# Masked-autoencoder loss: other column pieces and other PSUM tiles in the last columns

## The chip, the cores and the metric

The kernel runs on one core of a Trainium2 chip. The metric is the device time of one execution in microseconds (us). Of the kernel before, six runs are shown: 76.96 to 77.12, with a median of 77.03.

## The reference

`pred` and `target` are float32 arrays of 32 x 147 x 768 (batch, masked patches, values of a patch). Each patch of `target` is normalised by its own mean and variance, the squared difference to `pred` is averaged over the 768 values, and then over the 147 patches. The result is 32 numbers.

```python
mean = target.mean(axis=-1, keepdims=True)
var = target.var(axis=-1, keepdims=True)
target = (target - mean) / np.sqrt(var + 1e-6)
loss = np.mean((pred - target) ** 2, axis=-1)
return loss.mean(axis=-1).astype(np.float32)
```

## The kernel before

**Tiling.** Four partitions hold the patches of one batch entry, so 32 entries fill 128 partitions. A partition holds up to 37 patches, one after the other; the kernel calls each a column, 768 values wide. Columns 0 to 35 fill all 128 partitions. Column 36, called `REST`, has 96. `KM` is 36, `half` is 384, `BANK` is 512 and `D` is 768.

**Loads.** The list `stream` (lines 54 to 78) sets the order of the loads. Target comes in pieces of four columns, `pred` in pieces of four, then of two (columns 24 to 31), then of one (32 to 34); column 35 comes in two pieces of 384 values. Two target pieces are issued by SP, all else by POOL, whose transfers convert float32 to bfloat16. POOL issues a load between other work, in the order that the planner sets.

**Statistics and normalisation.** DVE takes mean and variance of a target column (lines 161 and 162), ACT the square root (185), DVE the reciprocal (191). POOL writes the normalised column into a tile `s` (line 211).

**Difference and square.** A unit is a stretch of one or two columns that is finished by one path. On the ACT path PE multiplies `s` by minus the identity into PSUM (`sub_target`, the operation `subt`, a subtraction), then adds `pred` by the identity (`add_pred`, the operation `pred`, an addition); both matmuls are on line 228. ACT squares the PSUM tile in place and sums it (line 249; the sum is read out by an ACTIVATION_READ_ACCUMULATOR). On the DVE path DVE subtracts (line 265) and squares with a sum (line 269), or leaves the square to ACT ("DVE+ACT").

From column 26 on each unit is divided. Columns 26 and 27, 28 and 29, 30 and 31 are pairs, and 32 to 35 are single. ACT takes the first part of a column's values, DVE the rest. The part of ACT is 512 values wide up to column 33, and 384 for columns 34 and 35 (lines 87 to 90). A pair's part is two matmuls of 512, a single column's is one.

**PSUM.** Whole pairs of columns up to 23 and `REST` use a pool of two tiles of three banks. When the first part is to be subtracted, that pool is closed and a pool `parts` of three tiles of two banks takes its place (lines 231 to 242). Every part takes the next of the three tiles, so it can be written only when the part three before it was squared: 32 waits for 26 and 27, 33 for 28 and 29, 34 for 30 and 31, and 35 for 32. The sum over partitions, `acc`, has a bank of its own.

**Order.** All operations are put into a list with an estimated duration, the operations that they need, a rank, and, where they need a transfer, its estimated landing. A planner (lines 336 to 356) takes again and again the operation that can start first by these estimates, and issues it. This fixes the program order of every engine. The estimates fix no time: on the chip an engine does its instructions in that order, each when its operands are there.

**End.** Squares of the last six units are summed one by one. The earlier ones stand side by side in `rl` and are reduced on DVE (`rl_sum`, line 321). PE multiplies each vector of sums by a mask into `acc` (line 328), DVE copies it (359), and SP stores it (360).

Of the kernel before, what the change touches and what calls it, by code (L numbers as in the profile page):

```python
# [7 lines left out]
F32 = mybir.dt.float32  # L8
# [6 lines left out]
def kernel(  # L15
# [9 lines left out]
    B, N, D = pred.shape  # L25
    eps = 1e-6
    P = 128
    J = P // B
    KJ = (N + J - 1) // J
    KM = N - (J - 1) * KJ  # L30
    assert KJ == KM + 1
    RP = B * (J - 1)
    half = D // 2
    BANK = 512
# [19 lines left out]
    def piece(kind, c0, c1, d0=0, d1=D, q="sw"):  # L54
        stream.append((kind, c0, c1, d0, d1, q))
# [18 lines left out]
        piece("p", c, c + 2)  # L74
    for c in range(32, 35):
        piece("p", c, c + 1)
    piece("p", KM - 1, KM, 0, half)
    piece("p", KM - 1, KM, half, D)


    groups = [(0, 1), (2, 3), (REST,)] + [tuple(range(c, c + 4)) for c in range(4, KM, 4)]
# [2 lines left out]
    units = [((c, c + 1), 0, D, "ACT" if c < 14 else "DVE+ACT") for c in range(0, 24, 2)]  # L84
    units.insert(2, ((REST,), 0, D, "ACT"))
    units += [((24,), 0, D, "DVE"), ((25,), 0, D, "DVE+ACT")]
    for u in [(c, c + 1) for c in range(26, KM - 4, 2)] + [(c,) for c in range(KM - 4, KM - 1)]:
        m = BANK if u[0] < KM - 2 else half
        units += [(u, 0, m, "ACT"), (u, m, D, "DVE")]
    units += [((KM - 1,), 0, half, "ACT"), ((KM - 1,), half, D, "DVE")]  # L90

# [3 lines left out]
    def op(name, engine, dur, needs, fn, rank=0.0, early=0.0):  # L97
        by_name[name] = len(ops)
        ops.append((name, engine, dur, needs, fn, rank, early))
# [17 lines left out]
    for i, (kind, c0, c1, d0, d1, q) in enumerate(stream):  # L117
        w = (c1 - c0) * (d1 - d0)
# [4 lines left out]
        k = len(lanes[q])  # L123
# [6 lines left out]
    ident = singles.tile([P, P], BF16)  # L130
# [71 lines left out]
    def normalise(u, c):  # L202
        n = rows_of(c)
        if c == u[0]:
            s = work.tile([P, 2 * D], BF16, name="s")
            for m, cc in enumerate(u):
                sbuf[cc] = (s, m * D)
        s, so = sbuf[c]
        (_, _, til, o), = tbuf[c]
        r, nm = rs[c]  # L210
        pin(nc.gpsimd.tensor_scalar(out=s[:n, so:so + D], in0=til[:n, o:o + D], scalar1=nm, scalar2=r,  # L211
                                    op0=ALU.add, op1=ALU.mult))


    zs = {}
# [5 lines left out]
    def product(u, d0, w, src, so, eye, first):  # L221
        n, z = rows_of(u[0]), zs[u, d0]

        runs = [(0, so, w)] if w % D == 0 else [(k * BANK, so + k * D, w // len(u)) for k in range(len(u))]
        for zo, o, e in runs:
            for a in range(0, e, BANK):
                b = min(e, a + BANK)
                pin(nc.tensor.matmul(z[:n, zo + a:zo + b], eye[:n, :n], src[:n, o + a:o + b],  # L228
                                     start=first, stop=not first))

    def sub_target(u, d0, w):
        if u in pairs_pe:
            zs[u, d0] = pools["pairs"].tile([P, 3 * BANK], F32, name="z")
            pairs_pe.remove(u)
        else:
            if "parts" not in pools:

                pools["stack"].close()
                pools["parts"] = ctx.enter_context(tc.tile_pool(name="parts", bufs=3, space=bass.MemoryType.PSUM))
            zs[u, d0] = pools["parts"].tile([P, 2 * BANK], F32, name="zp")  # L240
        s, so = sbuf[u[0]]
        product(u, d0, w, s, so + d0, nident, True)

    def add_pred(u, d0, w):
        product(u, d0, w, *pred_of(u[0], d0), ident, False)

    def square_act(u, d0, w, dest):
        n, z = rows_of(u[0]), zs[u, d0]
        pin(nc.scalar.activation(out=z[:n, :w], in_=z[:n, :w], func=ACTF.Square, accum_out=dest[:n]))  # L249

    def difference(u, d0, w):

        z = zs[u, d0] = diffs.tile([P, 2 * D], BF16, name="zd")
        s, so = sbuf[u[0]]
        til, o = pred_of(u[0], d0)
        K, e = len(u), w // len(u)
        if e == D:
            x, y, v = z[:, :w], til[:, o:o + w], s[:, so:so + w]
        elif K == 1:
            x, y, v = z[:, :w], til[:, o:o + w], s[:, so + d0:so + d0 + w]  # L260
        else:
            x = z[:, :w].rearrange("p (k d) -> p k d", d=e)
            y = til[:, o - d0:o - d0 + K * D].rearrange("p (k d) -> p k d", d=D)[:, :, d0:d0 + e]
            v = s[:, so:so + K * D].rearrange("p (k d) -> p k d", d=D)[:, :, d0:d0 + e]
        pin(nc.vector.tensor_tensor(out=x, in0=y, in1=v, op=ALU.subtract))  # L265

    def square_dve(u, d0, w, dest):
        z = zs[u, d0][:, :w]
        pin(nc.vector.scalar_tensor_tensor(out=z, in0=z, scalar=1.0, in1=z, op0=ALU.mult, op1=ALU.mult,  # L269
                                           accum_out=dest))  # L270
# [6 lines left out]
    n_pairs = len(pairs_pe)  # L277
    pools = {"stack": ExitStack()}
    pools["pairs"] = pools["stack"].enter_context(tc.tile_pool(name="psum", bufs=2, space=bass.MemoryType.PSUM))
    finals = []  # L280
    early_ops, users, dusers, dprev, seen = [], [], [], [], set()
    for k, (u, d0, d1, eng) in enumerate(units):
        w = len(u) * (d1 - d0)
        arrive = max(t for (kk, c, d), t in land.items() if kk == "p" and c in u and d < d1)
        norms = [("norm", c) for c in u]
        for c in u:
            if c not in seen:
                op(("norm", c), "POOL", 1.02, [("recip", group_of[c])], lambda u=u, c=c: normalise(u, c), rank=k)
                seen.add(c)
        if k < len(units) - tail:  # L290
            if u[0] == REST:
                dest = singles.tile([P, 1], F32, name="rl_rest")
                finals.append((("sq", k), dest, mask_rest, RP))
            else:
                dest = rl[:, len(early_ops):len(early_ops) + 1]
                early_ops.append(("sq", k))
        else:
            dest = singles.tile([P, 1], F32, name=f"rl{k}")
            finals.append((("sq", k), dest, mask, P))
        if eng in ("DVE", "DVE+ACT"):  # L300
            op(("diff", k), "DVE", 0.57 * w / D + 0.05, norms + dusers[-5:-4] + dprev[-1:], lambda u=u, d0=d0, w=w: difference(u, d0, w), rank=-2.0,
               early=arrive)
            dusers.append(("sq", k))
            dprev.append(("diff", k))
            if eng == "DVE":
                op(("sq", k), "DVE", 1.0 * w / D, [("diff", k)],
                   lambda u=u, d0=d0, w=w, dest=dest: square_dve(u, d0, w, dest), rank=-1.0)
            else:
                op(("sq", k), "ACT", 0.65 * w / D + 0.22, [("diff", k)],
                   lambda u=u, d0=d0, w=w, dest=dest: square_act(u, d0, w, dest), rank=k)  # L310
            continue
        op(("subt", k), "PE", 0.37 * w / D, norms + (users[-2:-1] if len(users) < n_pairs else users[n_pairs - 1:n_pairs] + users[n_pairs:][-3:-2]) + ["ident"],
           lambda u=u, d0=d0, w=w: sub_target(u, d0, w), rank=k + 0.0)
        op(("pred", k), "PE", 0.37 * w / D, [("subt", k)], lambda u=u, d0=d0, w=w: add_pred(u, d0, w), rank=k,
           early=arrive)
        op(("sq", k), "ACT", 0.65 * w / D + 0.22, [("pred", k)],
           lambda u=u, d0=d0, w=w, dest=dest: square_act(u, d0, w, dest), rank=k)
        users.append(("sq", k))

    acc = psum1.tile([1, B], F32)  # L320
    op("rl_sum", "DVE", 0.2, early_ops, lambda: pin(nc.vector.tensor_reduce(
# [18 lines left out]
    while left:  # L340
        best = None
        for i in left:
            name, engine, dur, needs, fn, rank, early = ops[i]
# [8 lines left out]
        name, engine, dur, needs, fn, rank, early = ops[i]  # L352
# [43 lines left out]
```

## Time and profile before

| what | before |
|---|---|
| median of six runs | 77.03 us |
| the profiled execution | 77.12 us |
| its span, first to last instruction | 75.4 us |
| PE busy | 28.9 us |
| DVE busy | 56.4 us |
| ACT busy | 30.3 us |
| POOL busy | 53.7 us |
| loads | 15.41 MB written, 28.90 MB read at 383 GB/s |
| mean granted TensorE clock | 0.769 |

The span ends with the last instruction; the time also holds what lies around the program. Busy time is a sum over the whole span, so an engine can be half idle and yet set the end. A line of the timeline gives the start, the duration, the engine, the line of the kernel and the operation, what it writes and reads, and in brackets how long its engine was idle before it and what ended that. The names of buffers leave their numbers out: `zp` is any tile of the pool `parts`, `zd` the output of the DVE's subtraction. The ends of matmuls are modelled: several in a row follow each other sooner than their durations say.

### The profile page before, as it was taken

The numbers are of one execution on the slowest core, as the hardware profiler recorded it, in microseconds if no ns is written. First come the engines' busy times: TensorE is split into PE (matmuls) and PEld (weight loads), VectorE is DVE, ScalarE is ACT, GpSimd is POOL, SyncE is SP. The second block draws the span as 40 slices with busy tenths as digits, with TensorE's granted clock in tenths as the row PEclk, the third lists the DMA queues.
The fourth block names the chain that finished last, engine by engine and source line by source line (L and its number), as shares of the span: only waits on it lengthen the run. The fifth ranks groups of instructions, "written<-read, shape, count | busy, mean of one in ns | idle before, by whom it ended". The sixth has DMA issues, their size and how long they took to land.

```text
span 75.4 us, 551 instructions
## 1 busy us (share of the span) xinstructions
PE 28.9 (38%) x81; PEld 8.3 (11%) x82; DVE 56.4 (75%) x155; ACT 30.3 (40%) x65; POOL 53.7 (71%) x75
## 2 busy tenths in 40 slices
PE   0000001472005876004986006770719300379860
PEld 0000000110002131001121002120103000112230
DVE  0000699999999979999759999375797289998860
ACT  5100021200102893020690010880099969965760
POOL 6998006997399949698989898997695999800000
PEclk9999999999999999995557965555555555555598
DMA  0799999999999999999999999999999999999700
GB/s 0 215 417 324 254 240 218 191 239 209 215 215 212 209 219 215 228 209 212 215 212 212 219 212 225 215 209 215 215 215 215 199 215 212 212 204 204 109 0 0
DMA packets 3685, 15.41 MB, mean 204 GB/s; under 512 B 418, under 2 KB 1154, under 8 KB 3554
## 3 DMA queue, kind: packets, MB, share of 16 engines
q0 software_dynamic: 3424, 13.52, 88.6%
q1 hardware_dynamic: 258, 1.87, 6.8%
q14 instruction: 3, 0.02, 0.1%
HBM read 28.90 MB, written 0.00 MB: 383 GB/s over the span
## 4 chain that ended last, share of the span: by engine, by line
DMA 60%; POOL 22%; DVE 5%; issue 3%; PE 3%; ACT 3%; ACTq 1%; POOLq 0%
DMA t<-in_target_dram 31%; DMA p<-in_pred_dram 29%; POOL s L211 15%; DVE st L161 4%; POOL p L111 4%; ACT zp L249 3%; PE zp L228 3%; POOL t L111 2%; ACTq L391 1%; DVE mv L162 1%; POOL nident L139 0%; POOL ident L139 0%; PE acc L328 0%; DVE ob L359 0%; POOL nident L138 0%
## 5 line engine op out<-in xcount | busy, mean ns | idle before, releaser
L161 DVE BATCH_NORM_STATS2 st<-t 128x6 f32<-128x384 bf16 (+2 forms) x74 | 36.2, 531 | 10.5 <-DMA t<-in_target_dram 10.5
L211 POOL TENSOR_SCALAR s<-t,nm,r 128x768 bf16<-128x768 bf16 (+2 forms) x37 | 38.3, 1043 | 5.6 <-DVE r L191 4.9
L228 PE MATMUL z<-p,ident 128*128 128x512 bf16 (+2 forms) x23 | 10.1, 596 | 19.1 <-DMA p<-in_pred_dram 19.1
L228 PE MATMUL z<-s,nident 128*128 128x512 bf16 (+2 forms) x23 | 9.8, 536 | 15.9 <-POOL s L211 14.3
L249 ACT ACTIVATE z<-z 128x1536 f32<-128x1536 f32 (+1 forms) x8 | 10.9, 1357 | 12.2 <-PE z L228 12.2
L185 ACT ACTIVATE r<-mv,eps_t 128x4 f32<-128x4 f32 (+2 forms) x11 | 3.2, 292 | 27.1 <-DVE mv L162 26.4
L265 DVE TENSOR_TENSOR zd<-p,s 128x1536 bf16<-128x1536 bf16 (+4 forms) x14 | 9.6, 702 | 3.6 <-DMA p<-in_pred_dram 3.5
L111 POOL DMA_DIRECT2D p<-in_pred_dram x16 | 9.1, 571 | 3.9 <-DMA t<-in_target_dram 1.2
L162 DVE BATCH_NORM_AGGREGATE mv<-st 128x2 f32<-128x12 f32 (+1 forms) x37 | 7.7, 209 | 1.3
L249 ACT ACTIVATE zd<-zd 128x1536 bf16<-128x1536 bf16 (+1 forms) x6 | 8.2, 1364 | 0.7 <-DVE zd L265 0.7
L228 PEld LDWEIGHTS <-ident 128*128 128x128 bf16 (+1 forms) x33 | 4.4, 135 | 34.6 <-issue 34.5
L228 PE MATMUL zp<-p,ident 128*128 128x512 bf16 (+1 forms) x9 | 4.4, 553 | 6.9 <-DMA p<-in_pred_dram 6.9
L228 PEld LDWEIGHTS <-nident 128*128 128x128 bf16 (+1 forms) x33 | 3.3, 121 | 29.1 <-issue 15.9
L249 ACT ACTIVATE zp<-zp 128x1024 f32<-128x1024 f32 (+2 forms) x7 | 5.2, 736 | 1.8 <-PE zp L228 1.8
L111 POOL DMA_DIRECT2D t<-in_target_dram x8 | 4.7, 612 | 1.5 <-DVE r L191 1.5
L228 PE MATMUL zp<-s,nident 128*128 128x512 bf16 (+1 forms) x10 | 5.0, 605 | 2.0 <-ACT z L249 1.7
L269 DVE SCALAR_TENSOR_TENSOR zd<-zd 128x512 bf16<-128x512 bf16 (+3 forms) x8 | 5.0, 624 | 0.2
L186 ACT ACTIVATE nm<-mv 128x4 f32<-128x4 f32 (+2 forms) x11 | 2.1, 189 | 0.0
L185 ACT ACT_TABLE_LOAD x1 | 1.3, 1283 | 0.8 <-PEq L377 0.8
L249 ACT ACTIVATION_READ_ACCUMULATOR z<-z 128x1 f32 (+1 forms) x8 | 1.5, 191 | 0.0
L191 DVE RECIPROCAL r<-r 128x4 f32<-128x4 f32 (+2 forms) x11 | 1.4, 124 | 0.1
L249 ACT ACTIVATION_READ_ACCUMULATOR zp<-zp 128x1 f32 x7 | 1.3, 189 | 0.0
(25 smaller groups left out, 6.8 us busy)
## 6 DMA issues: line engine op xcount, KB each, us to landing
t<-in_target_dram POOLq DMA_DIRECT2D x8, 768.0 KB, 24.6
p<-in_pred_dram POOLq DMA_DIRECT2D x6, 768.0 KB, 29.0
t<-in_target_dram SPq DMA_DIRECT2D x1, 1536.0 KB, 7.4
p<-in_pred_dram POOLq DMA_DIRECT2D x4, 384.0 KB, 24.5
p<-in_pred_dram POOLq DMA_DIRECT2D x3, 192.0 KB, 16.4
t<-in_target_dram SPq DMA_DIRECT2D x1, 288.0 KB, 10.5
p<-in_pred_dram POOLq DMA_DIRECT2D x2, 96.0 KB, 9.5
p<-in_pred_dram POOLq DMA_DIRECT2D x1, 144.0 KB, 13.2
```

The source lines that it names most:

```text
L111: pin(eng.dma_start(out=til[:n], in_=src))
L161: pin(nc.vector.bn_stats(out=st[:n, j, :], in_=x))
L162: pin(nc.vector.bn_aggr(out=out, in_=st[:n, :len(parts)]))
L185: pin(nc.scalar.activation(out=r[:n], in_=mv[:n, :, 1], func=ACTF.Sqrt, bias=eps_t[:n], scale=1.0))
L186: pin(nc.scalar.activation(out=nm[:n], in_=mv[:n, :, 0], func=ACTF.Copy, scale=-1.0))
L191: pin(nc.vector.reciprocal(out=rs[g][:n], in_=rs[g][:n]))
L211: pin(nc.gpsimd.tensor_scalar(out=s[:n, so:so + D], in0=til[:n, o:o + D], scalar1=nm, scalar2=r, op0=ALU.add, op1=ALU.mult))
L228: pin(nc.tensor.matmul(z[:n, zo + a:zo + b], eye[:n, :n], src[:n, o + a:o + b], start=first, stop=not first))
L249: pin(nc.scalar.activation(out=z[:n, :w], in_=z[:n, :w], func=ACTF.Square, accum_out=dest[:n]))
L265: pin(nc.vector.tensor_tensor(out=x, in0=y, in1=v, op=ALU.subtract))
L269: pin(nc.vector.scalar_tensor_tensor(out=z, in0=z, scalar=1.0, in1=z, op0=ALU.mult, op1=ALU.mult, accum_out=dest))
L391: with _tile.TileContext(nc) as tc:
```

## The change

Column 35 is loaded in pieces of 512 and 256 values instead of 384 and 384. Its parts, and those of column 34, are 512 for ACT and 256 for DVE, as in the columns before. The pool `parts` has two tiles of two banks, for the three pairs. A new pool `last` has three tiles of one bank (`zl`), for the single columns 32 to 35. The planner's needs follow: a pair's subtraction needs the square of the pair two before it, a single column's the square of the single column three before it. Everything else is as it was.

```diff
-    piece("p", KM - 1, KM, 0, half)
-    piece("p", KM - 1, KM, half, D)
+    piece("p", KM - 1, KM, 0, BANK)
+    piece("p", KM - 1, KM, BANK, D)
...
-        m = BANK if u[0] < KM - 2 else half
-        units += [(u, 0, m, "ACT"), (u, m, D, "DVE")]
-    units += [((KM - 1,), 0, half, "ACT"), ((KM - 1,), half, D, "DVE")]
+        units += [(u, 0, BANK, "ACT"), (u, BANK, D, "DVE")]
+    units += [((KM - 1,), 0, BANK, "ACT"), ((KM - 1,), BANK, D, "DVE")]
...
-                pools["parts"] = ctx.enter_context(tc.tile_pool(name="parts", bufs=3, space=bass.MemoryType.PSUM))
-            zs[u, d0] = pools["parts"].tile([P, 2 * BANK], F32, name="zp")
+                pools["parts"] = ctx.enter_context(tc.tile_pool(name="parts", bufs=2, space=bass.MemoryType.PSUM))
+                pools["last"] = ctx.enter_context(tc.tile_pool(name="last", bufs=3, space=bass.MemoryType.PSUM))
+            if len(u) == 2:
+                zs[u, d0] = pools["parts"].tile([P, 2 * BANK], F32, name="zp")
+            else:
+                zs[u, d0] = pools["last"].tile([P, BANK], F32, name="zl")
...
-    early_ops, users, dusers, dprev, seen = [], [], [], [], set()
+    early_ops, users, dusers, dprev, pusers, lusers, seen = [], [], [], [], [], [], set()
...
-        op(("subt", k), "PE", 0.37 * w / D, norms + (users[-2:-1] if len(users) < n_pairs else users[n_pairs - 1:n_pairs] + users[n_pairs:][-3:-2]) + ["ident"],
+        op(("subt", k), "PE", 0.37 * w / D, norms + (users[-2:-1] if len(users) < n_pairs else users[n_pairs - 1:n_pairs] + (pusers[-2:-1] if len(u) == 2 else lusers[-3:-2])) + ["ident"],
...
         users.append(("sq", k))
+        if len(users) > n_pairs:
+            (pusers if len(u) == 2 else lusers).append(("sq", k))
```

## The prediction

> **What bounds the kernel now.** I read the busy slices first: DMA engines are at 9 tenths from slice 2 to slice 36, POOL and DVE beside them. So the body runs at the pace of the loads, and an edit of the last columns can only move what comes after the last bytes. Then the chain that ended last; its last steps (start, us, what):
>
> ```profile
> 46.15 21.79 DMA p<-in_pred_dram
> ...
> 67.98 1.02 PE zp L228 x2
> ...
> 69.03 0.87 ACT zp L249
> ...
> 70.20 0.94 PE zp L228 x2
> ...
> 71.22 0.45 ACT zp L249
> ...
> 72.40 0.50 ACT zp L249 x2
> ...
> 72.95 0.29 PE acc L328 x4
> ```
>
> The loads hand over to PE, ACT, PE, ACT. The step at 70.20 is the one to look at: between two pieces of ACT work stands PE work that had to wait. Next the timeline of PE, ACT and DVE from 70 us (start, duration, engine, line, operation):
>
> ```profile
> 70.04 0.59 ACT L249 ACTIVATE zp<-zp 128x512 f32<-128x512 f32 x1
> 70.20 0.50 PE L228 MATMUL zp<-s,nident 128*128 128x384 bf16 x1 [0.35 <-ACT zp L249]
> 70.49 0.63 PE L228 MATMUL zp<-p,ident 128*128 128x512 bf16 x1
> 70.56 0.18 ACT L249 ACTIVATION_READ_ACCUMULATOR zp<-zp 128x1 f32 x1
> 70.79 0.10 PEld L228 LDWEIGHTS <-nident 128*128 128x128 bf16 x1 [0.47 <-ACT zp L249]
> 70.92 0.52 PE L228 MATMUL zp<-s,nident 128*128 128x384 bf16 x1
> 71.22 0.58 ACT L249 ACTIVATE zp<-zp 128x512 f32<-128x512 f32 x1 [0.48 <-PE zp L228]
> 71.24 0.54 PE L228 MATMUL zp<-p,ident 128*128 128x384 bf16 x2
> 71.72 0.19 ACT L249 ACTIVATION_READ_ACCUMULATOR zp<-zp 128x1 f32 x1
> 71.81 0.48 ACT L249 ACTIVATE zp<-zp 128x384 f32<-128x384 f32 x1
> 71.87 0.36 DVE L265 TENSOR_TENSOR zd<-p,s 128x384 bf16<-128x384 bf16 x1
> 72.30 0.48 ACT L249 ACTIVATE zp<-zp 128x384 f32<-128x384 f32 x1
> 72.71 0.19 ACT L249 ACTIVATION_READ_ACCUMULATOR zp<-zp 128x1 f32 x1
> 72.75 0.08 DVE L269 DVE_READ_ACCUMULATOR zd<-zd 128x1 f32 x1
> ```
>
> On PE the order is: subtract 34 (70.20, held until the square of columns 30 and 31 freed its tile), add 33 (70.49), subtract 35 (weights at 70.79, held by the square of 32, which ended at 70.56 + 0.18 = 70.74), then adds 34 and 35 (71.24). ACT lost 0.48 us because add 33 stood behind subtract 34. After that ACT is back to back and ends at 72.90; DVE ends at 72.83, bound by the last piece of `pred`: it started at 71.87 although it was free at 71.83. The issue of that piece is at 63.22, and the shorter of the two last landings takes 8.6 us: it lands at 71.82. The piece before it: 60.80 + 10.5 = 71.3.
>
> **The skill.** "TensorE: Matmul & The Clock Gate", "What's actually happening": PE runs at half clock until a free-running window of about 3.4 us was busy. The trace agrees. Its answer by stretches of time gives the length, then busy time and count of PE, PEld, DVE, ACT and POOL, then the granted clock:
>
> ```profile
> 67.90:71.33 3.43, 3.00 (x8) 0.87 (x8) 3.00 (x12) 2.19 (x7) 0.00 (x0) 0.50 1.01 170
> 71.33:73.50 2.17, 1.47 (x19) 0.63 (x17) 1.61 (x6) 1.57 (x6) 0.00 (x0) 1.00 0.01 1
> ```
>
> The clock is 0.50 from 44.0 on and rises near 71.33; 71.33 - 44.0 is 8 times 3.42. The windows 37.2:40.6 (2.99 busy) and this one (3.00) raised it, 47.4:50.8 (2.68) did not. The same page, "Single matmul latency", gives (219 + N)/1.2 ns at half clock and (398 + N)/2.4 at full: 609 and 379 ns for 512 columns; the trace has 0.63 for the first. "PSUM — Partial Sum Buffer", "Specifications (TRN2)": eight banks of 512 float32. Two tiles of two banks, three of one, and the bank of `acc` make 4 + 3 + 1 = 8: it fits, with none to spare. "ScalarE: Activation LUTs", "What ACT_TABLE_LOAD costs": 0.833 ns per element; 128 more cost 0.107, and the trace has 0.58 - 0.48 = 0.10.
>
> **The change, part by part.**
>
> *Order.* The planner issues the ready instruction with the earliest planned start. Three things on PE have to be followed; add and subtraction carry the number of their column, 34 for column 34. (1) Subtractions 32, 33 and 34 no longer wait for an older square, only for their normalised rows; they go ahead of add 26, into PE's idle time before 64.25 (5.17 us idle there). POOL's last but one normalisation ends at 61.41 + 1.86 = 63.27, plus 0.63 of matmul is 63.9: add 26 is not delayed, with 0.3 to spare; without it everything on ACT would shift by the excess. (2) Subtraction 30 now waits for the square of 26 (ends 65.43 + 1.00, read out at 66.55); it takes the place that subtraction 32 has now (66.91) with two matmuls of 0.42, free at 67.75, before the piece for add 30 lands at 67.94. Hidden, with 0.2 to spare. (3) Subtraction 35 still waits for the square of 32, which is the old owner of its tile. In the planner's figures that square ends at 69.62, so subtraction 35 is ready at 69.77, and piece 34 is due at 70.10: subtraction 35 stays ahead of add 34 on the in-order PE. This is the important line. No load moves, and POOL's and SP's queues keep their order.
>
> *What add 33 gains.* Its piece lands near 69.93 (DVE starts its difference at 69.95). Nothing stands before it now: 70.0 + 0.65 to 0.73 is ready by 70.7, so the square of 33 follows that of 32 almost at once, at 70.65 in place of 71.22: 0.57 earlier.
>
> *What the sizes cost.* Square 32 still ends at 70.74, because its start is set by square 30, and that by the load at 67.94. Subtraction 35: weights at 70.79, matmul at 70.80 (PE is now free; today it stood behind add 33 until 70.92). It has 512 columns in place of 384, so the next matmul follows 0.41 later (67.98 to 68.79 has two in 0.81) and not 0.32 (70.92 to 71.24). Add 34 starts at 71.21, with 512 columns at half clock: 0.63 to its end, 0.03 to 0.10 to ACT (both occur): square 34 starts at 71.90, in place of 71.81. The 0.57 gained before is lost to an idle ACT. Square 34 takes 0.59 to the next start (as 71.22 to 71.81): square 35 at 72.49. Its data are there: piece 35a has 128 columns more, 66 KB at 383 GB/s is 0.17, so it lands at 71.47, ahead of add 35 at 71.62. Square 35 ends after 0.69 (71.22 to 71.91): 73.18. Against 72.90 that is +0.28: 0.09 from the later start, 0.10 from the wider square 34 (0.59 to the next start, not 0.49) and 0.09 from the wider square 35 (0.69, not 0.60).
>
> *DVE.* Two differences and squares of 256 columns instead of 384. Square 34 ends before the last piece lands; from 71.87 the pair takes 0.75 (69.14 to 69.89): 72.62, 0.21 earlier than today and 0.56 before ACT. Worth nothing while ACT ends later. Should the narrower last piece land late, it has 0.5 of cover.
>
> *Clock.* In the window to 71.33 PE loses subtractions 33 and 34; four matmuls of about 0.42 and 0.54 us of subtraction 35 and add 34 are left, 2.25 of streaming against 2.8 now (2.3 in the window that did not raise it). With drains counted, as the busy column does, it is 2.80, between 2.68 and 3.00. I take it that the clock stays at half. The last four small matmuls (0.28 at full clock) then cost some 0.03 more, by the page's two formulas at 32 columns (209 against 179 ns).
>
> Sum: 0.28 + 0.03 = +0.31. The profiled execution took 77.12 with a span of 75.4, so 77.43 for such a one; the median of the runs shown is 77.03, 0.09 lower, and gives **77.34 us**. What a measurement of this kernel can tell from no change is about 0.2%, 0.15 us.
>
> **Rivals.**
>
> *B, the clock still rises at 71.33.* Add 34 streams 0.13 at half and the rest at full clock, ends at 71.67; squares start at 71.72 and 72.31, end at 72.99: +0.09, 77.12. For it: 2.80 busy is near 3.00. Against: the streamed time.
>
> *C, the other side: the clock rises before 70.8.* The window is free-running, so another execution can cut it elsewhere. From 66.11 the changed PE is nearly solid for 3.4 us: two adds, two subtractions, two adds, one add, 7 x 0.42 = 2.9. A window that begins between 65.7 and 66.4 has 2.6 or more and gives full clock from about 69.5. Subtraction 35 at 70.80, add 34 at 71.02, square 34 at 71.46, square 35 at 72.05, end 72.74: -0.16, 76.87. It decides when the clock is full before 70.8. For it: the trace shows how sharply windows switch. Against: 0.7 of 3.4 positions is a fifth, and a median wants more.
>
> *D, subtraction 35 is not in the way* (placed behind add 34, or its tile free sooner). Square 34 then starts 0.69 after the landing of piece 34 near 70.85, at 71.54; square 35 at 72.16, end 72.85: -0.05 at half clock, -0.28 at full. Against: 69.77 before 70.10 in the plan.
>
> *E, the new tiles free nothing*, because they come to wait with the old ones: only the sizes act. Subtraction 34 70.20, add 33 70.62, subtraction 35 71.04, add 34 71.46, squares 72.15 and 72.74, end 73.43: +0.53, 77.56; +0.32 with the clock rising as now. Also here: early subtractions that delay add 26.
>
> **How the numbers follow.** The forecast, A, has 0.55, its own range 77.20 to 77.48 from the readings 0.03 to 0.10, 0.65 to 0.73 and 0 to 0.07 for the end; B 0.17; C 0.13; D 0.06; E 0.09. Slower by over 0.2%: A 0.53 + E 0.08 = 0.61. Within: A 0.02, E 0.01, B 0.16, C 0.06, D 0.02 = 0.27. Faster: C 0.07, D 0.04, B 0.01 = 0.12. The range 76.85 to 77.50 holds most of A, all of B, half of C and of D.
>
> **What would show it.** Right: subtractions of 512 columns on PE between 60 and 64 us; square 33 starts within 0.1 of the end of square 32; then an idle ACT of about 0.5 us put down to PE; weights for subtraction 35 at the end of square 32; DVE done half a microsecond before ACT; clock 0.50 to the end. Wrong: add 34 before subtraction 35, a clock of 1.00 before 71, ACT without that gap, or add 26 later than 64.3.

## The result, and the profile after

| | before | changed |
|---|---|---|
| median | 76.94 us (65 executions) | 77.24 us (29 executions) |
| lowest to highest | 76.61 to 77.28 | 76.72 to 77.58 |
| ratio of the times | | 1.0026, 95% interval 1.0014 to 1.0037 |

The changed kernel is slower by a quarter of a percent: 0.20 us by the ratio, 0.30 us between the medians. The two numbers differ because its times are not one cloud. Twelve of the 29 lie at 76.72 to 76.98, seventeen at 77.22 to 77.58, and none between. With a second series of 14 and two single executions (below) there are 18 in the lower group, median 76.79, and 27 in the upper, median 77.31. Against 76.94 that is -0.15 and +0.37 us. The times of before are spread without such a gap.

The first profile of the changed kernel happens to be one of the lower group: 76.79 us, span 75.1. Read alone against the 75.4 of before it would tell the wrong story. These are its lines in the timeline that answer to those shown of before, and the copy of the result on DVE (start, duration, engine, line, operation):

```profile
70.40 0.58 ACT L252 ACTIVATE zl<-zl 128x512 f32<-128x512 f32 x1
...
70.55 0.39 PE L227 MATMUL zl<-s,nident 128*128 128x512 bf16 x1 [0.62 <-ACT zl L252]
...
70.78 0.78 PE L227 MATMUL zl<-p,ident 128*128 128x512 bf16 x2
70.91 0.18 ACT L252 ACTIVATION_READ_ACCUMULATOR zl<-zl 128x1 f32 x1
...
71.19 0.58 ACT L252 ACTIVATE zl<-zl 128x512 f32<-128x512 f32 x1
...
71.78 0.59 ACT L252 ACTIVATE zl<-zl 128x512 f32<-128x512 f32 x1
...
72.29 0.19 ACT L252 ACTIVATION_READ_ACCUMULATOR zl<-zl 128x1 f32 x1
...
72.94 0.18 DVE L364 COPY ob<-acc 1x32 f32<-1x32 f32 x1 [0.62 <-PE acc L333]
```

And the same stretch in an execution of the upper group, 77.29 us, the run `look_b`:

```profile
68.83 1.01 ACT L252 ACTIVATE zp<-zp 128x1024 f32<-128x1024 f32 x1 [0.81 <-PE zp L227]
...
70.44 0.59 ACT L252 ACTIVATE zl<-zl 128x512 f32<-128x512 f32 x1
...
70.60 0.61 PE L227 MATMUL zl<-s,nident 128*128 128x512 bf16 x1 [0.40 <-ACT zl L252]
...
70.96 0.18 ACT L252 ACTIVATION_READ_ACCUMULATOR zl<-zl 128x1 f32 x1
...
71.00 1.06 PE L227 MATMUL zl<-p,ident 128*128 128x512 bf16 x2
...
71.67 0.58 ACT L252 ACTIVATE zl<-zl 128x512 f32<-128x512 f32 x1 [0.53 <-PE zl L227]
...
72.25 0.59 ACT L252 ACTIVATE zl<-zl 128x512 f32<-128x512 f32 x1
...
72.77 0.19 ACT L252 ACTIVATION_READ_ACCUMULATOR zl<-zl 128x1 f32 x1
...
73.01 0.37 PE L333 MATMUL acc<-mask,rl 128*1 128x32 f32 x4 [0.22 <-ACT zl L252]
73.42 0.18 DVE L364 COPY ob<-acc 1x32 f32<-1x32 f32 x1 [1.04 <-PE acc L333]
```

Up to subtraction 35 (the first PE line of each) the two differ by 0.05 us. That subtraction begins as the square of 32 is read out (70.36 + 0.19 = 70.55 in `look_b`). Then one matmul of 512 columns takes 0.40 to the next in `look_b` and 0.23 in the first profile, and the first add behind it reaches ACT 0.67 and 0.41 after its start. ACT idles 0.53 in one and 0.10 in the other before square 34 (71.67 against 70.96 + 0.18, and 71.19 against 70.91 + 0.18). The rest follows on ACT alike. The answer by stretches, for 70.5 to 71.5 us, gives the clock as the third figure from the right, in the first profile and then in `look_b`:

```profile
70.50:71.50 1.00, 0.93 (x4) 0.23 (x5) 0.80 (x4) 0.90 (x3) 0.00 (x0) 1.00 0.50 67
```

```profile
70.50:71.50 1.00, 0.90 (x3) 0.28 (x3) 0.81 (x4) 0.64 (x3) 0.00 (x0) 0.50 0.49 64
```

### The profile page after: what moved, and what is told of

Read it like the earlier page. It is cut to its first block, busy times and chain, and to the rows that moved or that the text cites. A ratio compares the mean times of both kernels' runs of the same rounds, so it can differ in the third digit from the quotient of the medians.

```text
span 75.1 us, 549 instructions
## 1 busy us (share of the span) xinstructions
PE 29.4 (39%) x81; PEld 8.3 (11%) x82; DVE 55.9 (74%) x155; ACT 30.6 (41%) x65; POOL 53.7 (72%) x75
## 4 chain that ended last, share of the span: by engine, by line
DMA 53%; POOL 28%; issue 6%; PE 5%; ACT 3%; ACTq 1%; DVE 0%; POOLq 0%
DMA p<-in_pred_dram 31%; DMA t<-in_target_dram 22%; POOL s L210 21%; PE zp L227 4%; POOL p L110 4%; POOL t L110 2%; ACT zl L252 2%; ACT zp L252 1%; PE zl L227 1%; ACTq L396 1%; PE acc L333 1%; POOL ident L138 0%; POOL nident L138 0%; DVE ob L364 0%; POOL nident L137 0%
## 5 line engine op out<-in xcount | busy, mean ns | idle before, releaser
L268 DVE TENSOR_TENSOR zd<-p,s 128x1536 bf16<-128x1536 bf16 (+3 forms) x14 | 9.5, 687 | 3.8 <-DMA p<-in_pred_dram 3.7
L272 DVE SCALAR_TENSOR_TENSOR zd<-zd 128x256 bf16<-128x256 bf16 (+2 forms) x8 | 4.7, 590 | 0.2
L227 PE MATMUL zl<-s,nident 128*128 128x512 bf16 x4 | 2.1, 536 | 4.5 <-POOL s L210 3.9
L227 PE MATMUL zp<-s,nident 128*128 128x512 bf16 x6 | 2.9, 627 | 1.7 <-ACT z L252 1.7
L252 ACT ACTIVATE zp<-zp 128x1024 f32<-128x1024 f32 x3 | 3.0, 1006 | 1.4 <-PE zp L227 1.4
L227 PE MATMUL zp<-p,ident 128*128 128x512 bf16 x5 | 2.6, 603 | 1.7 <-DMA p<-in_pred_dram 1.7
L252 ACT ACTIVATE zl<-zl 128x512 f32<-128x512 f32 x4 | 2.3, 586 | 0.1
L227 PE MATMUL zl<-p,ident 128*128 128x512 bf16 x4 | 1.7, 416 | 0.4 <-DMA p<-in_pred_dram 0.4
```

## The experiments

The theory to test, W: in the tail PE waits for old squares with an add behind it, and what that costs is set by the TensorE clock. Rivals: S, the wider squares on ACT are the whole loss; T, the new PSUM tiles cost something themselves.

### The two halves of the change, one at a time

`sizes_only` is the kernel before with the sizes of the change alone:

```diff
-    piece("p", KM - 1, KM, 0, half)
-    piece("p", KM - 1, KM, half, D)
+    piece("p", KM - 1, KM, 0, BANK)
+    piece("p", KM - 1, KM, BANK, D)
...
-        m = BANK if u[0] < KM - 2 else half
+        m = BANK
...
-    units += [((KM - 1,), 0, half, "ACT"), ((KM - 1,), half, D, "DVE")]
+    units += [((KM - 1,), 0, BANK, "ACT"), ((KM - 1,), BANK, D, "DVE")]
```

> Only the sizes are changed (512 and 256 for columns 34 and 35, and for the last piece of pred); the PSUM pool stays as before. Theory W (PE's wait for old squares, at half clock): subtractions 34 and 35 both wait and both are 512 wide, so executions with the TensorE clock at half in the last 3 us take 0.3 to 0.5 us more than before, those with the full clock about 0.1 less; mean +0.2 to +0.3. Rival S (only the wider squares on ACT cost, 2 x 0.10): +0.2 to +0.3 in every execution, in one cluster. Rival T (the new PSUM tiles cost): 0.

Measured: 77.59 us against 77.00, ratio 1.0074 (1.0058 to 1.0090). That is +0.57 us; the prediction had +0.53 for this case at half clock. The cluster that W expected 0.1 us below the kernel before did not appear: six executions, the lowest at 77.25. Its profile, ACT and PE:

```profile
70.90 0.63 PE L228 MATMUL zp<-s,nident 128*128 128x512 bf16 x1
71.20 0.58 ACT L249 ACTIVATE zp<-zp 128x512 f32<-128x512 f32 x1 [0.59 <-PE zp L228]
71.32 1.06 PE L228 MATMUL zp<-p,ident 128*128 128x512 bf16 x2
...
72.05 0.58 ACT L249 ACTIVATE zp<-zp 128x512 f32<-128x512 f32 x1 [0.17 <-PE zp L228]
...
72.64 0.59 ACT L249 ACTIVATE zp<-zp 128x512 f32<-128x512 f32 x1
```

ACT waits for PE twice, 0.59 before square 33 and 0.17 before square 34. The clock was at half up to about 72.5 in this execution.

`psum_only` is the other half: the changed kernel with `half` put back in these lines.

> Only the PSUM tiles and the order of the subtractions are changed; columns 34 and 35 keep 384 and 384. W: ACT ends about 0.1 us earlier in either clock, DVE's last part still starts at the landing of the last piece and takes 0.96, so the end moves by -0.07 us, in one cluster, whatever the clock. S: 0 to -0.1. T: slower, +0.2 or more.

Measured: 76.87 us, ratio 0.9988 (0.9981 to 0.9996), 21 executions in one group from 76.75 to 77.07. So -0.09 us for a forecast of -0.07: little, but the interval lies below 1. T falls: the new tiles and the earlier subtractions cost nothing. In its profile ACT ends at 72.51 and DVE at 72.54, with the clock at half. DVE's last part of 384 columns began at 71.59, with no idle time before it, and ends last, so it limits the gain. By the ratios the halves add to +0.48; the whole at half clock, the upper group, is +0.37. It is not a plain sum: from the start of square 30 to the end of ACT the new tiles bring 0.17 us with the narrow parts (3.70 in `psum_only`, 3.87 in before) and 0.32 with the wide ones (4.13 in `look_b`, 4.45 in `sizes_only`).

### Taking away the wait of subtraction 35

`sub35_free` lets column 35 use the two-bank tile that columns 28 and 29 leave:

```diff
-            if len(u) == 2:
+            if len(u) == 2 or u[0] == KM - 1:
...
-(pusers[-2:-1] if len(u) == 2 else lusers[-3:-2])
+(pusers[-2:-1] if len(u) == 2 or u[0] == KM - 1 else lusers[-3:-2])
```

> As the changed kernel, but subtraction 35 writes the two-bank tile that columns 28 and 29 leave free at about 68.3 us, so that it does not wait for the square of 32 and goes ahead of add 32. W: add 34 starts at the landing of its piece; -0.05 us against the kernel before at half clock, -0.2 to -0.3 at full clock, and the ACT gap before square 34 is under 0.3 us. S: the wider squares stay, so +0.2 to +0.3 against before.

Measured: 76.72 us, ratio 0.9968 (0.9956 to 0.9980). The profile is of an execution at half clock:

```profile
70.45 0.59 PE L227 MATMUL zl<-p,ident 128*128 128x512 bf16 x1 [0.37 <-DMA p<-in_pred_dram]
70.84 0.18 ACT L252 ACTIVATION_READ_ACCUMULATOR zl<-zl 128x1 f32 x1
71.08 0.58 ACT L252 ACTIVATE zl<-zl 128x512 f32<-128x512 f32 x1
```

Add 34 is released by the transfer now, not by ACT's square, and ACT idles 0.06 us instead of 0.53. The squares are as wide as in the changed kernel, and yet it is faster than the kernel before: S falls. Run once more, as `cold_free35`:

> The kernel with the free tile for subtraction 35 again, on another chip run, to fix its ratio: -0.2 to -0.3 us against the kernel before, at either clock, so one group within 0.3 us.

Measured: 76.80 us, ratio 0.9983 (0.9970 to 0.9995), from 76.60 to 77.02 over 14 executions. The gain is there again but smaller, -0.14 where -0.2 was the least expected, and the spread is 0.42, not 0.3: of the six executions with a mean granted clock of 0.77 five lie above 76.9, and the eight with 0.80 to 0.83 all lie below. The two profiles say where the gain is. From the start of square 30 to the copy of the result before takes 4.24 us (69.03 to 73.27). `sub35_free`, at half clock, takes 4.24 as well (68.71 to 72.95), and `cold_free35`, with the clock full from 69.13 on, takes 4.01 (68.86 to 72.87). So in these two profiles the free tile makes the wider squares cost nothing at half clock, and brings 0.2 at full clock. The clock still matters here, by less than in the changed kernel, and without a gap.

`add34_first` keeps the wait but puts subtraction 35 behind add 34 (its needs gain `("pred", k - 2)`).

> As the changed kernel, but subtraction 35 comes after add 34 in PE's order; it still waits for the square of 32. W: at half clock square 34 starts about 0.35 earlier than in the changed kernel, then ACT waits for add 35: +0.15 against before; at full clock -0.2. S: as the changed kernel, +0.2 to +0.3.

Measured: 77.13 us, ratio 1.0007 (0.9993 to 1.0021): not to be told from before by the ratio, because there are two groups again, five executions at 76.56 to 76.89 and seventeen at 77.05 to 77.36. Its profile is of the upper group, at half clock: square 34 starts at 71.41, 0.04 after the read-out of square 33, and square 35 at 72.32 after 0.23 us of waiting for add 35. The wait has moved one column on, as W said, and the upper group, median 77.15, is 0.15 above before instead of 0.37.

### The clock

The two groups were expected to be two states of the TensorE clock. First the changed kernel again:

> The changed kernel again, unedited, for a second profile. W: its executions fall into two groups, near 76.85 and near 77.3 us, with a gap of about 0.2 between them; in a profile of the later group the clock is 0.50 until at least 71 us, ACT idles 0.6 to 0.7 us before square 34 (end of its predecessor's read-out to its start), and the copy of the result starts about 0.4 later than in the first profile.

Measured: six executions at 76.68 to 76.79 with a mean granted clock of 0.795 to 0.831, eight at 77.26 to 77.51 with 0.744 to 0.773. The ratio of this series is 1.0017 (0.9993 to 1.0042). The profile was again of the lower group (clock 1.00 from about 68.56 us to the end), so what was said of the upper one was left to two more executions:

> The changed kernel, one look for its profile. W: if its time is above 77.1 the clock is 0.50 until 71 us at least and ACT idles about 0.5 us before square 34; if it is below 77.0 the clock is 1.00 at 70.5 us and the idle time is about 0.1.

> The changed kernel, one more look, with the same expectation: above 77.1 the clock is 0.50 until 71 us at least and ACT idles about 0.5 us before square 34; below 77.0 the clock is 1.00 at 70.5 us and the idle time is about 0.1.

Both lay above: 77.43 and 77.29 us, clock 0.50 from 66 to the end of the program, ACT idle 0.53 in each (the second series' expectation had 0.6 to 0.7). The mean clock of `look_a` over the span is 0.807, as high as in the lower group, although the clock was 0.50 from 53.4 us on. The mean counts all time before the first recorded change as full clock: up to 39.7 us in `look_a`, up to 26.3 in `look_b`. The matmuls do not bear that out: six of 512 columns at 23.69 in `look_a` take 2.72 us, as six do at 34.65 in `look_b`, where the record has 0.50. So the clock has to be read in the last stretch; a mean over the span can hide it.

These are sightings. Two edits move the clock. `clock_down` leaves out one subtraction:

```diff
-        product(u, d0, w, s, so + d0, nident, True)
+        if u[0] != 30:
+            product(u, d0, w, s, so + d0, nident, True)
```

(the add of these columns then starts the tile).

> As the changed kernel, but the two matmuls that subtract columns 30 and 31 are left out (the loss of these parts is then computed without target), so PE is 0.85 us less busy between 66.5 and 67.7 us; every other instruction keeps its place. W with the clock as the cause of the two groups of times: no 3.4 us window is busy enough any more, the clock stays at half to the end, and all executions lie with the slower group, 77.2 to 77.6 (about +0.35 us against before), none under 77.1. If the groups have another cause (loads, landing times): both groups stay, 76.7 to 77.0 and 77.2 to 77.6.

Measured: 77.35 us, ratio 1.0044 (1.0027 to 1.0060), eight executions from 77.14 to 77.57, none of them in the lower group. With less work on PE the kernel is by its ratio slower than the changed kernel itself, though the two intervals overlap. Its profile repeats `look_b`: ACT idles 0.53 before square 34, and the clock is 0.50 to the end.

```profile
71.62 0.58 ACT L253 ACTIVATE zl<-zl 128x512 f32<-128x512 f32 x1 [0.53 <-PE zl L227]
```

`clock_up` adds six matmuls (`acc` becomes a part of the bank that they write):

```diff
-    acc = psum1.tile([1, B], F32)
+    wide = psum1.tile([P, BANK], F32, name="wide")
+    acc = wide[0:1, 0:B]
...
+    def warm():
+        s, so = sbuf[32]
+        pin(nc.tensor.matmul(wide, ident, s[:, so:so + BANK], start=True, stop=True))
...
+    for k, n in ((15, 3), (19, 1), (21, 1), (23, 1)):
+        for i in range(n):
+            op(("warm", k, i), "PE", 0.01, [("norm", 32), ("warm", k, i - 1) if i else ("pred", k)], warm, rank=-100.0)
```

> As the changed kernel, with six added matmuls of 512 columns that nobody reads, in PE's idle time: three behind add 26, one each behind adds 30, 32 and 33. W with the clock as the cause: the window before 70.5 us is busy in nearly every execution, the clock is full for subtraction 35 and adds 34 and 35, and nearly all executions lie at 76.7 to 77.0, -0.15 us against before. Otherwise: the two groups stay, or the added matmuls delay the adds and all is slower.

Measured: 76.86 us, ratio 0.9983 (0.9967 to 0.9998), twelve executions of which eleven lie at 76.70 to 77.03 and one at 77.14. The group at 77.22 and above is gone. Its profile has the clock at 1.00 from 66.84 us on:

```profile
70.28 0.39 PE L227 MATMUL zl<-s,nident 128*128 128x512 bf16 x1
70.64 0.19 ACT L252 ACTIVATION_READ_ACCUMULATOR zl<-zl 128x1 f32 x1
70.66 0.38 PE L227 MATMUL zl<-p,ident 128*128 128x512 bf16 x1
71.08 0.58 ACT L252 ACTIVATE zl<-zl 128x512 f32<-128x512 f32 x1 [0.25 <-PE zl L227]
```

Subtraction 35 starts at 70.28, and a matmul of 512 columns keeps the next one waiting 0.23 us at full clock, so PE is free before add 34 at 70.66. It still waits for the square of 32, but square 30 itself came earlier at full clock. Work that nobody reads made the kernel faster, by raising the clock of work that somebody waits for.

`sub35_free_clock_up` joins the free tile and five such matmuls.

> The free tile for subtraction 35 together with five added matmuls (three behind add 26, one each behind adds 32 and 33). W: add 34 follows its landing at full clock, ACT ends about 72.6 and DVE too, so -0.25 to -0.3 us against before, in one group. If the clock did not matter: as with the free tile alone.

Measured: 76.71 us, ratio 0.9951 (0.9928 to 0.9974), seven executions from 76.55 to 76.81. This is the fastest version: -0.31 us by the medians, -0.38 by the ratio, against its own runs of before, where -0.25 to -0.3 was expected. Its interval overlaps that of the free tile alone in the first series, so what the added matmuls are worth on top of the free tile is not settled. In their series both versions beat both kernels.

## Why the prediction was right, and where it was off

**The order on PE** came out as read from the plan: subtractions 32, 33 and 34 in the idle time before add 26 (59.57, 60.53 and 62.98 us in the first profile), subtraction 30 ahead of its add without delaying it, subtraction 35 ahead of add 34.

**The mechanism of the forecast** is what the upper group does, term by term. Measured from the start of square 30, so that the loads' own shift between executions drops out:

| term | forecast | `look_b` |
|---|---|---|
| subtraction 35 to add 34 | 0.41 | 0.40 |
| add 34 to square 34 | 0.69 | 0.67 |
| end of ACT against before | +0.28 | +0.26 (72.96 - 68.83 against 72.90 - 69.03) |
| last squares to the copy, against before | +0.03 | +0.09 (0.46 against 0.37) |
| sum | +0.31 | +0.35 |

The copy of before, for the row before the last:

```profile
73.27 0.18 DVE L359 COPY ob<-acc 1x32 f32<-1x32 f32 x1 [0.44 <-PE acc L328]
```

The end is the mis-sized term: at half clock the last four small matmuls take 0.37 (73.01) where they took 0.28, and the wait ahead of them did not shrink. The prediction took 0.03 from two formulas for a single bf16 matmul; these are four float32 matmuls in a chain.

**DVE** ended 0.59 before ACT in `look_b` (72.29 + 0.08 against 72.96), as the prediction said (0.56): its narrower parts were worth nothing. They matter only where ACT is no longer late: in `psum_only` DVE, with its part of 384, ends last by 0.03, and in `sub35_free`, with 256, it ends 0.22 before ACT (72.26 against 72.48).

**Rival C was no rival but the other half of the truth.** The prediction gave it 0.13 as a case in which the whole measurement goes the other way, and priced it at -0.16. Its mechanism and its size were right, -0.15. What failed is the step from the mechanism to its weight: "a window that begins between 65.7 and 66.4 has 2.6 or more", and so a fifth of the positions. The share was 18 of 45, two in five. Loads land at other times in every execution, so positions are counted here from the start of the first matmul of add 28, 66.11 in before; the prediction's stretch is then -0.4 to +0.3. The windows that raised the clock in the two profiles of the lower group begin at -0.26 in the first and at -0.61 in `changed_again` (65.55 and 65.15, from the rise at 68.96 and 68.56 less 3.41; add 28 at 65.81 and 65.76): one inside the stretch, one ahead of it. The window of `changed_again` holds six matmuls of 512 columns, at 0.42 each 2.5 us of streaming. The window 67.03 to 70.45 of `look_a`, in the upper group, holds 5.4 of them, 2.3 us, and did not raise the clock. But six are not always enough either: the windows 65.70 to 69.11 of `sizes_only` and 67.48 to 70.89 of `sub35_free` hold six and did not. So the point from which it decides lies close to six matmuls, and what tips the balance there stays open. The weight hangs on it: with six in place of 2.6 us, which is a little more than six, the stretch grows in the prediction's own times from 0.7 to about 1.55 of 3.41 (65.4 to 66.95), near half of all positions. That is an estimate, and close to the share that was seen.

And since executions cut the window differently, the case should have been put into a mixture: a median of two groups, 0.5 us apart, of which the upper has the majority. That is why the measured 77.24 lies 0.10 under the forecast, at the lower edge of the upper group. That the median fell there is in part luck: with three more of the 29 executions in the lower group it would have been under 77.0.

**Rival B** (the clock rises at 71.33 as in the profile of before) was not seen: in `look_a` and `look_b` the windows to 70.45 and 70.62 (counted in steps of 3.41 from earlier switches) did not raise the clock, and no execution of the 45 lies between 76.98 and 77.22, where its +0.09 falls. **Rival D** put two things under one price, and only one of them is worth it. With its tile free sooner, subtraction 35 is out of the way: from the start of square 30 to the end of ACT `sub35_free` takes 3.77 us at half clock and `cold_free35` 3.56 at full, against 3.87, so -0.10 and -0.31 where -0.05 and -0.28 were priced. Placed behind add 34 it holds up add 35 instead, and `add34_first` takes 3.94, +0.07. **Rival E** (only the sizes act) was priced at +0.53 and the edit gave +0.57.

What stays open: why `sizes_only` had no lower group in six executions. Its PE work sits at other times, and six are few.

## What to carry to other kernels

Where an engine keeps its program order, as PE's matmuls do here, ask of every wait what stands behind it: in `look_b` square 33 starts 1.61 us after square 30, where it took 2.19, and these 0.58 us were lost again because the fourth subtraction still waited, with the next add behind it. Taking PE work out of the tail can take the clock from the tail, as `clock_down` shows: count what is left in the last window before calling a moved matmul free. And if a small change shows two groups of times, look for a profile of each before explaining either.

## What the runs showed of the hardware

One profile does not stand for a kernel whose TensorE clock switches: of four profiled executions of the same program two ran subtraction 35 and adds 34 and 35 at half clock and two at full clock. "TensorE: Matmul & The Clock Gate", "What's actually happening", says that the window is free-running. The profiles agree: each recorded stretch of the clock that ends inside a profile is a multiple of 3.41 us, and the cuts fall at another place in each. Here that is worth 0.5 us at the end of a 77 us kernel.

The busy column of the profile is a poor measure of what raises the clock. It counts the modelled end of each matmul, so that single matmuls with gaps look busier than they are. A window of `changed_again` with six matmuls close together, 2.80 busy, raised it (first line); one of `look_a`, with gaps between the matmuls, 2.93 busy, did not (second line):

```profile
65.15:68.56 3.41, 2.80 (x6) 0.80 (x6) 3.12 (x8) 2.17 (x5) 0.29 (x1) 0.50 1.10 206
```

```profile
67.03:70.45 3.42, 2.93 (x6) 0.51 (x4) 3.00 (x10) 2.60 (x5) 0.00 (x0) 0.50 1.17 205
```

Counted as columns streamed, at 0.42 us for 512, the two are 2.5 and 2.3 us, in the right order. That count is better and still not sharp: the window of `sub35_free` named above has six matmuls, 2.5 us, and 3.01 busy, and did not raise it.

Six added matmuls of 512 columns, on an engine that is busy 39% of the span in the changed kernel, changed the time by -0.17% against before, where the changed kernel had +0.26%, and left none of twelve executions in the upper group.
